# Head of a two-block transformer kernel: sums of squares and the first quarter of the modulation on TensorE, both factors of x in one VectorE pass, later sums before the second mixer

## The chip, the core and the metric

The kernel runs on 1 NeuronCore of one Trainium2 chip. The metric is device time in microseconds (us) of one execution; less is better. The engines named below are TensorE (PE in the profile; its weight loads are PEld), VectorE (DVE), ScalarE (ACT), GpSimd (POOL) and SyncE (SP), whose queue issues most of the transfers from memory.

## The reference, cut to what matters

Two transformer blocks run one after the other on 512 tokens of 1024 channels. What the change touches is the very first step, the normalised and modulated input of the first mixer, and the first product with it; and, far later, the norm that stands before the second mixer of the second block.

```python
c_act = jax.nn.silu(c)
mod = c_act @ ada_w[l] + ada_b[l]                 # 1024 -> 6 * 1024
shift1, scale1, gate1, shift2, scale2, gate2 = jnp.split(mod, 6)
h = rmsnorm(x, norm1_g[l]) * (1.0 + scale1) + shift1      # x: 512 x 1024
proj = h @ w_in[l]
...
def rms_norm(x, g):
    y = x * lax.rsqrt(jnp.mean(x * x, axis=-1, keepdims=True) + EPS)
    return y * g
...
x = x + rms_norm(sq_relu_mlp(h, ...), norm_mlp_post[0])   # second block, layer 0
m = mixer_c(rms_norm(x, norm_mix_pre[1]), ...)            # layer 1
```

## The kernel before, in words

Tokens lie along the free dimension and channels on the 128 partitions, so x is eight chunks (k = 0 to 7) of 128 channels by 512 tokens. Every product is made of three float32r matmuls: a weight slab and the activations are each split into a high part (a rounded copy, made on ACT) and a low part (the rest, made on DVE), and `mm3` issues high by high, high by low and low by high. A split of a weight slab is one ACT cast (`w_hi`, L168) and one DVE subtraction (`w_lo`, L169) of 128x1024.

**The head** is `first_products`. In it the order on every engine is the order in which the code is written (`manual_schedule`). It loads x and the columns of `ada_w` that give shift1 and scale1, in four quarters q: a quarter is eight tiles of 128x512 (k = 0 to 7, two to a buffer of 128x1024) and gives shift and scale for the chunks 2q and 2q+1. `ada` multiplies a quarter's tiles by c_act on DVE and adds them up over k; `columns` sums the result over the partitions with matmuls of one column (four for each 128x512 tile, 128x128 float32 weights, a column of ones as the moving side), and makes the factors `mod`. The squares of x are made on ACT, added up over k on DVE (L648) and summed over the partitions by four matmuls (`col_sum`, L326); the square root is a power on POOL (L344, `rs_r`); four matmuls `spread` it to 128 partitions (L353) and ACT copies it out (`rstd`, L356). Then x is multiplied by rstd (L654, chunk 0 on DVE, the others on POOL), by its scale factor on ACT (L636), and the shift is added while it is split in h_hi (ACT, L638) and h_lo (DVE, L639).

The first five products then grow side by side in five PSUM tiles: two slabs, the narrow forget slab `fa`, two more slabs. `mm(n, q)` adds slab n's share of quarter q, six matmuls of 512 columns. After slab number `NAT` of a quarter the next quarter's columns and factors stand in PE's order.

One float32 matmul leaves two records in the trace: "x8" in a row of L326, L353, L628 or L1320 is four matmuls.

**Before the second mixer** the last MLP product of layer 0 is made in two halves of 256 tokens (`halves`). The tail of a half (`post`) is woven between the matmuls of what follows, one step for each step or two of the other work: it makes the sums of squares of the new x (DVE, L283), then waits `late` steps, then sums them over the partitions on PE (L326, `csum`), takes the power on POOL (L1552, `mix_rcol`) and, two steps later, spreads it on PE (L1557). `LATE[1]` holds the late steps of the first and of the second half. POOL also adds the squares of the MLP's output m (L283 on POOL) in this stretch, and the scheduler orders this part itself.

Of the kernel before, what the change touches and what calls it, by code (L numbers as in the profile page):

```python
# [9 lines left out]
F32 = mybir.dt.float32  # L10
# [3 lines left out]
AF = mybir.ActivationFunctionType  # L14
OP = mybir.AluOpType
# [4 lines left out]
P = 128  # L20
S = 512
# [28 lines left out]
RATE = 1.0  # L50
APB = 2
EV = 1000
NPE = 0
NAT = 1
GY = 2
VK = 1
PK = 1
# [1 line left out]
R1 = 0.4  # L59
R5 = 0.4  # L60
APP = 0
LATE = ((40, 22), (34, 10))

# [19 lines left out]
class Net:  # L83
# [503 lines left out]
    def first_products(self, w, evacs, tmp, nf, rows):  # L587

        nc = self.nc
        with ExitStack() as es:  # L590
            sp = self.pool(es, "start", side="right")
            self.dense(es, 4)
            pp = self.pool(es, "pstart", 3, space=PSUM)
            more = [lambda: sp.tile([P, self.WN], F32, name="more_raw", bufs=2)] * 2
            self.weights_extra(self.zraw + more)
            self.parts.extend(self.pairs(sp, 2))
            E = mybir.EngineType
            es.enter_context(self.tc.manual_schedule(engines={E.PE, E.DVE, E.Activation, E.SP, E.Pool}))
# [12 lines left out]

            def ada(raws):
                acc = [sp.tile([P, 512], F32, name="ada_sum", bufs=4) for i in range(2)]
                for k in range(NC - NPE):
                    ck, a = self.c_act[:, k:k + 1], acc[k % 2]
                    if k < 2:
                        nc.vector.tensor_scalar(a, raws[k], ck, None, op0=OP.mult)
                    else:
                        nc.vector.scalar_tensor_tensor(a, raws[k], ck, a, op0=OP.mult, op1=OP.add)
                nc.vector.tensor_add(acc[0], acc[0], acc[1])  # L620
                return acc[:1]

            def columns(q, raws, acc):
                src = [(raws[k], self.c_act[:, k:k + 1]) for k in range(NC - NPE, NC)]
                for l, r in src + [(a, self.ones[:, :1]) for a in acc]:
                    for c in range(4):
                        d = 8 * (c // 2) + 2 * q + c % 2
                        nc.tensor.matmul(pa[:, d:d + 1], l[:, c * P:(c + 1) * P], r, start=False, stop=True,  # L628
                                         skip_group_check=True)
                for k in (2 * q, 2 * q + 1):  # L630
                    nc.scalar.mul(self.mod[:, 8 + k:9 + k], pa[:, 8 + k:9 + k], self.v("norm1_g", k))
                nc.scalar.copy(self.mod[:, 2 * q:2 * q + 2], pa[:, 2 * q:2 * q + 2])

            def modulate(q):
                for k in (2 * q, 2 * q + 1):
                    nc.scalar.mul(x[:, k], x[:, k], self.mod[:, 8 + k:9 + k])  # L636
                    b = self.mod[:, k:k + 1]
                    nc.scalar.activation(self.h[0][:, k], x[:, k], AF.Identity, bias=b)  # L638
                    nc.vector.scalar_tensor_tensor(self.h[1][:, k], x[:, k], b, self.h[0][:, k], op0=OP.add,  # L639
                                                   op1=OP.subtract)  # L640

            raws = [fetch(0)]
            acc = sp.tile([P, S], F32, name="acc", tag="ada_sum", bufs=4)
            nc.scalar.square(acc, x[:, 0])
            for k in range(1, NC):
                sq = sp.tile([P, S], F32, name="sq", bufs=2)
                nc.scalar.square(sq, x[:, k])
                nc.vector.tensor_add(acc, acc, sq)  # L648
            c = sp.tile([P, 4], F32, name="rs_c")
            nc.scalar.activation(c, self.col_sum([acc]), AF.Identity, bias=self.eps, scale=1.0 / D)  # L650
            r = self.spread(self.rsqrt(c), sp)
            sums = [ada(raws[0])]
            for k in range(NC):
                (nc.gpsimd if k else nc.vector).tensor_mul(x[:, k], x[:, k], r)  # L654
            slabs = [self.slab(w[i], NC) for i in range(2)]
            raw = sp.tile([P, NC * 16], F32, name="fa_raw")
            nc.sync.dma_start(raw, self.t["w_fa"])
            fa = tuple(sp.tile([P, NC, 16], F32R, name=n) for n in ("fa_h", "fa_l"))
            rv = raw.rearrange("p (k c) -> p k c", k=NC)
            nc.scalar.copy(fa[0], rv)  # L660
            nc.vector.tensor_sub(fa[1], rv, fa[0])
            slabs.append(fa)
            raws.append(fetch(1))
            columns(0, raws[0], sums[0])
            modulate(0)
            sums.append(ada(raws[1]))
            slabs += [self.slab(w[i], NC) for i in (2, 3)]
# [8 lines left out]
            for q in range(4):  # L676
                if q < 2:
                    raws.append(fetch(q + 2))
                    sums.append(ada(raws[q + 2]))
                for n in range(5):  # L680
                    if q < 3:
                        mm(n, q)
                        if n == NAT:
                            columns(q + 1, raws[q + 1], sums[q + 1])
                            modulate(q + 1)
# [1615 lines left out]
```

## Time and profile before

| | |
|---|---|
| time before, median of 3 runs | 2283.05 us (2279.7 to 2284.46) |
| profiled execution, its own time | 2282.78 us |
| its span | 2281.1 us |
| instructions | 31923 |
| mean granted TensorE clock | 0.975 |
| busy share: PE, DVE, ACT, POOL | 95%, 61%, 49%, 19% |

The span is the stretch between the first and the last instruction, and about 1.7 us of the execution's time lie outside it. Shares are means over a long kernel of many stages; the head is its first 69 us, 3% of the span.

### The profile page before, as it was taken

What the parts mean: (1) busy time and instruction counts of PE and PEld (TensorE: products, weight loads), DVE (VectorE), ACT (ScalarE), POOL (GpSimd) and SP (SyncE); (2) the same over time, 40 slices, a digit from 0 to 9 for tenths busy, and PEclk for the clock granted to TensorE, in tenths of its full rate; (3) what the DMA queues carried; (4) which work ended last, traced back from release to release, by engine and by line L of the source; (5) the groups of instructions that cost most, each with busy time, mean ns of one, the idle gap of its engine ahead of it and who ended that gap; (6) DMA issues with size and microseconds to landing.
All of it is one profiled execution on the core that took longest, in us unless ns stands there. A gap on an engine that the chain in (4) does not pass through costs nothing. (4 is left out here: it accounts for less than half of the span.)

```text
span 2281.1 us, 31923 instructions
## 1 busy us (share of the span) xinstructions
PE 2167.1 (95%) x12164; PEld 1809.7 (79%) x12164; DVE 1393.0 (61%) x2002; ACT 1109.9 (49%) x1856; POOL 422.6 (19%) x468
## 2 busy tenths in 40 slices
PE   5999999979999999899999999999999999999996
PEld 4778778967888788678998888997666689888886
DVE  8577775568999964666543344565767846344343
ACT  3545542348888854445553233443655647332231
POOL 4111000231111142110400000350324433000004
PEclk9999999989999989999999999999999999999998
DMA  6464265569999741224332222342122142332321
GB/s 242 140 185 118 88 204 164 184 223 345 353 358 355 270 154 45 69 78 151 100 111 97 98 94 100 110 135 55 49 71 54 43 158 89 117 101 93 101 74 38
DMA packets 127154, 320.08 MB, mean 140 GB/s; under 512 B 24751, under 2 KB 30127, under 8 KB 126994
## 3 DMA queue, kind: packets, MB, share of 16 engines
q1 hardware_dynamic: 111934, 286.56, 36.8%
q0 software_dynamic: 11200, 22.91, 4.2%
q10 hardware_dynamic: 3860, 8.51, 1.0%
q8 instruction: 97, 1.59, 0.3%
q14 instruction: 63, 0.52, 0.1%
HBM read 296.31 MB, written 18.69 MB: 138 GB/s over the span
## 5 line engine op out<-in xcount | busy, mean ns | idle before, releaser
L196 PE MATMUL acc<-h_hi,w_hi 128*128 128x512 f32 (+1 forms) x1464 | 515.7, 352 | 3.5 <-DVE q L429 1.5
L200 PE MATMUL acc<-h_hi,w_lo 128*128 128x512 f32 (+1 forms) x1464 | 509.1, 348 | 1.2 <-DVE w_lo L169 1.2
L199 PE MATMUL acc<-h_lo,w_hi 128*128 128x512 f32 (+1 forms) x1464 | 508.7, 348 | 0.0
L169 DVE TENSOR_TENSOR w_lo<-x_raw,w_hi 128x1024 fp32r<-128x1024 f32 x260 | 317.8, 1231 | 189.8 <-ACT w_hi L168 185.2
L168 ACT CAST w_hi<-x_raw 128x1024 fp32r<-128x1024 f32 x260 | 271.0, 1046 | 283.8 <-PE acc L199 246.6
L196 PEld LDWEIGHTS acc<-h_hi,w_hi 128*128 128x128 f32 x1464 | 279.5, 191 | 36.9 <-issue 2.7
L200 PEld LDWEIGHTS acc<-h_hi,w_lo 128*128 128x128 f32 x1464 | 278.9, 190 | 35.9 <-DVE w_lo L169 2.5
L199 PEld LDWEIGHTS acc<-h_lo,w_hi 128*128 128x128 f32 x1464 | 279.0, 191 | 29.7 <-issue 0.7
L169 DVE TENSOR_TENSOR w_lo<-w_raw,w_hi 128x1024 fp32r<-128x1024 f32 (+2 forms) x141 | 166.8, 1184 | 145.0 <-ACT w_hi L168 141.3
L168 ACT CAST w_hi<-w_raw 128x1024 fp32r<-128x1024 f32 (+2 forms) x141 | 143.6, 1019 | 222.1 <-PE acc L199 199.3
L196 PE MATMUL acc<-act_hi,w_hi 128*128 128x512 f32 (+1 forms) x640 | 223.0, 349 | 0.0
L199 PE MATMUL acc<-act_lo,w_hi 128*128 128x512 f32 (+1 forms) x640 | 222.6, 348 | 0.0
L200 PE MATMUL acc<-act_hi,w_lo 128*128 128x512 f32 (+1 forms) x640 | 222.4, 348 | 0.0
L283 POOL TENSOR_TENSOR acc<-acc,sq 128x256 f32<-128x256 f32 x60 | 55.5, 926 | 721.0 <-ACT sq L282 720.2
L196 PEld LDWEIGHTS acc<-act_hi,w_hi 128*128 128x128 f32 x640 | 121.9, 190 | 15.3 <-ACT act_hi L1621 0.3
L199 PEld LDWEIGHTS acc<-act_lo,w_hi 128*128 128x128 f32 x640 | 121.9, 190 | 15.0
L200 PEld LDWEIGHTS acc<-act_hi,w_lo 128*128 128x128 f32 x640 | 121.8, 190 | 15.0
L506 DVE TENSOR_TENSOR pl<-pexp,ph 128x512 fp32r<-128x512 f32 x144 | 113.9, 803 | 25.9 <-ACT ph L505 25.1
L1626 DVE TENSOR_TENSOR m<-m,acc 128x512 f32<-128x512 f32 (+1 forms) x64 | 35.2, 552 | 138.7 <-PE acc L200 138.7
L470 DVE TENSOR_REDUCE mx<-acc 128x1 f32<-128x128 f32 x192 | 89.2, 484 | 37.9 <-PE acc L469 36.3
L504 ACT ACTIVATE pexp<-sT 128x512 f32<-128x512 f32 x144 | 82.5, 573 | 32.2 <-PE sT L495 14.2
L196 PE MATMUL gu<-w_hi,xh 128*128 128x512 f32 x240 | 95.5, 398 | 0.0
(593 smaller groups left out, 4422.0 us busy)
## 6 DMA issues: line engine op xcount, KB each, us to landing
x_raw<-mlp_w SPq DMA_DIRECT2D x90, 512.0 KB
w_raw<-mlp_w SPq DMA_DIRECT2D x48, 512.0 KB
x_raw<-w_down SPq DMA_DIRECT2D x40, 512.0 KB
x_raw<-w_up SPq DMA_DIRECT2D x39, 512.0 KB
x_raw<-w_gate SPq DMA_DIRECT2D x38, 512.0 KB
w_raw<-w_in SPq DMA_DIRECT2D x20, 512.0 KB
h_raw<-w_up SPq DMA_DIRECT2D x19, 512.0 KB
h_raw<-w_gate SPq DMA_DIRECT2D x18, 512.0 KB
```

What stands on the lines that cost most here:

```text
L168: nc.scalar.copy(hi[:, :n], raw[:, :n])
L169: (eng or nc.vector).tensor_sub(lo[:, :n], raw[:, :n], hi[:, :n])
L196: mm(ps, l[0], r[0], start=start, stop=False)
L199: mm(ps, l[0], r[1], start=False, stop=False)
L200: return mm(ps, l[1], r[0], start=False, stop=stop).ins
L283: (eng or nc.gpsimd).tensor_add(acc[:, a:a + 256], acc[:, a:a + 256], sq)
L470: self.last_max = nc.vector.reduce_max(mx[:, c0 + qb:c0 + qb + 1], ps[:, :n], axis=AX.X).ins
L504: nc.scalar.activation(e[:, :o], ps[:, :o], AF.Exp)
L506: nc.vector.tensor_sub(pt[1][:, :o], e[:, :o], pt[0][:, :o])
L1626: nc.vector.tensor_add(self.m[:, i, tok], self.m[:, i, tok], ps)
```

## The change

At the head, PE sums the squares of each chunk as ACT makes it (32 matmuls of one column that add in one PSUM tile, which a matmul with zeros opens), and PE makes the whole first quarter of the modulation from the raw tiles (c_act as the moving column), half of it ahead of the spread and half behind it. DVE multiplies x by the scale factor and rstd in one instruction (`scale`); the passes on POOL and ACT are gone. Of the later quarters PE takes three of eight tiles raw (`NPE = 3`) and DVE five. `NAT` becomes one number for each quarter, the factors and splits of the next two chunks stand behind `columns`, and the next quarter's DVE sums behind them. The slabs 2 and 3 are loaded ahead of quarter 1. Before the second mixer the late steps go from 34 and 10 to 44 and 14.

```diff
-NPE = 0
-NAT = 1
+NPE = 3
+NAT = (3, 2, 2)
-LATE = ((40, 22), (34, 10))
+LATE = ((40, 22), (44, 14))
...
-            def columns(q, raws, acc):
-                src = [(raws[k], self.c_act[:, k:k + 1]) for k in range(NC - NPE, NC)]
-                for l, r in src + [(a, self.ones[:, :1]) for a in acc]:
+            def columns(q, raws, ks, acc=()):
+                for l, r in [(raws[k], self.c_act[:, k:k + 1]) for k in ks] + [(a, self.ones[:, :1]) for a in acc]:
...
-            def modulate(q):
-                for k in (2 * q, 2 * q + 1):
-                    nc.scalar.mul(x[:, k], x[:, k], self.mod[:, 8 + k:9 + k])
...
+            def scale(k):
+                nc.vector.scalar_tensor_tensor(x[:, k], x[:, k], self.mod[:, 8 + k:9 + k], r, op0=OP.mult, op1=OP.mult)
...
-            for k in range(1, NC):
+            cs = self.pn.tile([P, S], F32, name="csum", tag=self.ntags[0])[:, :4]
+            nc.tensor.matmul(cs, self.zb, self.zb[:, :4], start=True, stop=True)
+            for k in range(NC):
                 sq = sp.tile([P, S], F32, name="sq", bufs=2)
                 nc.scalar.square(sq, x[:, k])
-                nc.vector.tensor_add(acc, acc, sq)
+                for j in range(4):
+                    nc.tensor.matmul(cs[:, j:j + 1], sq[:, j * P:(j + 1) * P], self.ones[:, :1], start=False, stop=True,
+                                     skip_group_check=True)
...
-            sums = [ada(raws[0])]
-            for k in range(NC):
-                (nc.gpsimd if k else nc.vector).tensor_mul(x[:, k], x[:, k], r)
-            slabs = [self.slab(w[i], NC) for i in range(2)]
+            columns(0, raws[0], range(4))
+            r = self.spread(c, sp)
+            columns(0, raws[0], range(4, NC))
+            mods(0)
+            scale(0)
+            scale(1)
+            parts(0)
+            slabs = [self.slab(w[0], NC)]
+            parts(1)
+            slabs.append(self.slab(w[1], NC))
...
+                    mm(n, q)
+                    if n == NAT[q]:
+                        columns(q + 1, raws[q + 1], range(NC - NPE, NC), sums)
+                        mods(q + 1)
+                        for k in (2 * q + 2, 2 * q + 3):
+                            scale(k)
+                            parts(k)
+                        if q < 2:
+                            sums = ada(raws[q + 2])
```

On PE, at the start of the program, the difference of the two orders reads as follows; csum holds the sums of squares, w_raw and x_raw the raw tiles of the first quarter, ada_sum the sums that DVE made, pst the first product.

```order
 L602 MATMUL acc<-ones,idf 128x8
-L326 MATMUL csum<-ones,acc 128x1 x4
+L646 LDWEIGHTS zb
+L646 MATMUL csum<-zb 128x4
+L651 MATMUL csum<-ones,sq 128x1 x32
+L627 MATMUL acc<-c_act,w_raw 128x1 x16
 L353 MATMUL spread<-idf,rs_r 128x128 x4
-L628 MATMUL acc<-ones,ada_sum 128x1 x4
+L627 MATMUL acc<-c_act,x_raw 128x1 x16
 L196 MATMUL pst<-h_hi,w_hi 128x512
```

Ahead of the first product stood 12 matmuls of one column or 128, now there are 68, and the spread stands behind 16 of them.

On DVE, in the order of the changed kernel alone, this is what stands between the constants and the sums for quarter 2 (L636 is the multiplication by both factors, L641 the low part of h, L617 to L620 the sums of a quarter).

```order
L636 SCALAR_TENSOR_TENSOR x<-x,mod,rstd 128x512 x2
L641 SCALAR_TENSOR_TENSOR h_lo<-x,mod,h_hi 128x512
L169 TENSOR_TENSOR w_lo<-x_raw,w_hi 128x1024
L641 SCALAR_TENSOR_TENSOR h_lo<-x,mod,h_hi 128x512
L169 TENSOR_TENSOR w_lo<-x_raw,w_hi 128x1024
...
L620 TENSOR_TENSOR ada_sum<-ada_sum 128x512
L636 SCALAR_TENSOR_TENSOR x<-x,mod,rstd 128x512
L641 SCALAR_TENSOR_TENSOR h_lo<-x,mod,h_hi 128x512
L636 SCALAR_TENSOR_TENSOR x<-x,mod,rstd 128x512
L641 SCALAR_TENSOR_TENSOR h_lo<-x,mod,h_hi 128x512
```

In the later quarters the scaling of the second chunk stands behind the low part of the first, which waits for ACT's high part.

On POOL, before the second mixer, the first half's power (mix_rcol) stood here between the sums of squares of m (acc<-acc,sq); this is the order before:

```order
L1498 DMA x_dram<-x 128x8x256
L283 TENSOR_TENSOR acc<-acc,sq 128x256 x3
L1552 TENSOR_TENSOR mix_rcol<-rs_c,mh 128x2
L283 TENSOR_TENSOR acc<-acc,sq 128x256 x2
L1763 MEMSET v_hi 128x32
```

and this the order of the changed kernel, where its line is L1563:

```order
L1509 DMA x_dram<-x 128x8x256
L283 TENSOR_TENSOR acc<-acc,sq 128x256 x5
L1563 TENSOR_TENSOR mix_rcol<-rs_c,mh 128x2
L1774 MEMSET v_hi 128x32
```

Two more sums now stand ahead of the power. On PE, 30 more matmuls of 256 columns stand between the tail's first spread and these sums over the partitions (149, before 119), and 6 instead of 11 between them and the spread of the power; in the second half, 96 instead of 48 matmuls of the next product stand ahead of the first of these sums.

## Rows read from the trace of the kernel before

**Rows 1.** The page, busy time of each engine: busy us, share, instructions.
```profile
PE 2167.1 (95%) x12164; PEld 1809.7 (79%) x12164; DVE 1393.0 (61%) x2002; ACT 1109.9 (49%) x1856; POOL 422.6 (19%) x468
```
**Rows 2.** Waits of PE: us in total, times, longest.
```profile
PE csum L326 <- DVE acc L648: 10.3, 1, 10.3
...
PE csum L326 <- DVE acc L283: 5.1, 2, 3.1
...
PE acc L628 <- DVE ada_sum L620: 4.2, 1, 4.2
PE pst L199 <- DVE h_lo L639: 4.0, 2, 3.5
```
**Rows 3.** Timeline of PE, head: start, length, what, [idle before].
```profile
17.89 2.07 PE L353 MATMUL spread<-idf,rs_r 128*128 128x128 f32 x8 [1.81 <-POOL rs_r L344]
19.76 1.81 PE L628 MATMUL acc<-ones,ada_sum 128*128 128x1 f32 x8
24.47 0.80 PE L196 MATMUL pst<-h_hi,w_hi 128*128 128x512 f32 x1 [2.90 <-ACT h_hi L638]
...
33.35 0.40 PE L200 MATMUL pst<-h_hi,w_lo 128*128 128x512 f32 x1
...
39.69 0.59 PE L196 MATMUL pst<-h_hi,fa_h 128*16 128x512 f32 x1
...
49.05 0.95 PE L628 MATMUL acc<-ones,ada_sum 128*128 128x1 f32 x8
49.86 0.40 PE L196 MATMUL pst<-h_hi,fa_h 128*16 128x512 f32 x1
...
68.73 0.28 PE L196 MATMUL acc<-w_hi,h_hi 128*128 128x256 f32 x1
```
**Rows 4.** Windows, head: busy us of PE, PEld, DVE, ACT, POOL, then PEclk, DMA.
```profile
39.00:43.00 4.00, 4.00 (x12) 2.35 (x13) 4.00 (x8) 3.07 (x7) 0.00 (x0) 0.50 0.91 303
```
**Rows 5.** Timeline of the other engines, head.
```profile
5.80 0.63 ACT L644 ACTIVATE acc<-x 128x512 f32<-128x512 f32 x1 [2.77 <-DMA x<-x]
...
16.47 1.37 POOL L344 TENSOR_TENSOR rs_r<-rs_c,mh 128x4 f32<-128x4 f32 x1 [4.18 <-DMA x_raw<-w_in]
...
20.49 1.99 ACT L168 CAST w_hi<-x_raw 128x1024 fp32r<-128x1024 f32 x2
...
23.70 0.72 ACT L638 ACTIVATE h_hi<-x,mod 128x512 fp32r<-128x512 f32 x1
...
39.86 0.41 ACT L631 ACTIVATE mod<-acc,vec 128x1 f32<-128x1 f32 x2 [12.20 <-PE acc L628]
...
59.68 0.75 DVE L639 SCALAR_TENSOR_TENSOR h_lo<-x,mod,h_hi 128x512 fp32r<-128x512 f32 x1 [5.64 <-ACT h_hi L638]
...
65.79 1.23 DVE L169 TENSOR_TENSOR w_lo<-w_raw,w_hi 128x1024 fp32r<-128x1024 f32 x1 [1.64 <-ACT w_hi L168]
```
**Rows 6.** Timeline of PE in another stage: matmuls of two columns.
```profile
826.07 2.72 PE L1320 MATMUL gu<-gg,sq 128*128 128x2 f32 x12 [0.84 <-ACT sq L1318]
828.65 0.77 PE L1313 MATMUL acc<-kept 128*128 128x256 f32 x2
```
**Rows 7.** Windows of that stage, columns as in rows 4.
```profile
828.00:830.00 2.00, 2.00 (x11) 2.00 (x11) 0.54 (x2) 0.83 (x2) 0.00 (x0) 0.50 0.44 166
```
**Rows 8.** Timeline before the second mixer, PE, POOL and DVE.
```profile
1477.23 0.56 PE L326 MATMUL csum<-ones,acc 128*128 128x1 f32 x2 [3.08 <-DVE acc L283]
...
1479.73 1.54 POOL L283 TENSOR_TENSOR acc<-acc,sq 128x256 f32<-128x256 f32 x2 [0.19 <-ACT sq L282]
1481.22 0.71 POOL L1552 TENSOR_TENSOR mix_rcol<-rs_c,mh 128x2 f32<-128x2 f32 x1
...
1509.65 1.23 DVE L169 TENSOR_TENSOR w_lo<-w_raw,w_hi 128x1024 fp32r<-128x1024 f32 x1
```
**Rows 9.** Windows before the second mixer, columns as in rows 4.
```profile
1477.00:1484.00 7.00, 6.41 (x29) 6.14 (x30) 2.53 (x6) 2.18 (x7) 4.65 (x5) 0.52 0.86 281
1511.00:1518.00 7.00, 7.00 (x35) 6.92 (x34) 4.89 (x9) 2.65 (x7) 4.07 (x10) 0.51 0.91 271
```

More of the change, by code (lines that the diff above doesn't have):

```diff
@@ L612, in ada @@
             def ada(raws):
-                acc = [sp.tile([P, 512], F32, name="ada_sum", bufs=4) for i in range(2)]
+                acc = [sp.tile([P, S], F32, name="ada_sum", bufs=4) for i in range(2)]
                 for k in range(NC - NPE):
@@ L629, in columns, with mods @@
                                          skip_group_check=True)
+            def mods(q):
                 for k in (2 * q, 2 * q + 1):
@@ L632, in columns @@
                 nc.scalar.copy(self.mod[:, 2 * q:2 * q + 2], pa[:, 2 * q:2 * q + 2])
-            def modulate(q):
-                for k in (2 * q, 2 * q + 1):
-                    nc.scalar.mul(x[:, k], x[:, k], self.mod[:, 8 + k:9 + k])
[L637 to L640, printed above, removed]
+            def scale(k):
+                nc.vector.scalar_tensor_tensor(x[:, k], x[:, k], self.mod[:, 8 + k:9 + k], r, op0=OP.mult, op1=OP.mult)
@@ L642, in first_products, with parts @@
+            def parts(k):
+                b = self.mod[:, k:k + 1]
+                nc.scalar.activation(self.h[0][:, k], x[:, k], AF.Identity, bias=b)
+                nc.vector.scalar_tensor_tensor(self.h[1][:, k], x[:, k], b, self.h[0][:, k], op0=OP.add,
+                                               op1=OP.subtract)
             raws = [fetch(0)]
-            acc = sp.tile([P, S], F32, name="acc", tag="ada_sum", bufs=4)
-            nc.scalar.square(acc, x[:, 0])
-            for k in range(1, NC):
+            cs = self.pn.tile([P, S], F32, name="csum", tag=self.ntags[0])[:, :4]
@@ L646, in first_products @@
+            nc.tensor.matmul(cs, self.zb, self.zb[:, :4], start=True, stop=True)
+            for k in range(NC):
                 sq = sp.tile([P, S], F32, name="sq", bufs=2)
                 nc.scalar.square(sq, x[:, k])
-                nc.vector.tensor_add(acc, acc, sq)
+                for j in range(4):
+                    nc.tensor.matmul(cs[:, j:j + 1], sq[:, j * P:(j + 1) * P], self.ones[:, :1], start=False, stop=True,
+                                     skip_group_check=True)
             c = sp.tile([P, 4], F32, name="rs_c")
-            nc.scalar.activation(c, self.col_sum([acc]), AF.Identity, bias=self.eps, scale=1.0 / D)
@@ L651, in first_products @@
-            r = self.spread(self.rsqrt(c), sp)
-            sums = [ada(raws[0])]
-            for k in range(NC):
-                (nc.gpsimd if k else nc.vector).tensor_mul(x[:, k], x[:, k], r)
-            slabs = [self.slab(w[i], NC) for i in range(2)]
+            nc.scalar.activation(c, cs, AF.Identity, bias=self.eps, scale=1.0 / D)
+            c = self.rsqrt(c)
+            columns(0, raws[0], range(4))
+            r = self.spread(c, sp)
+            columns(0, raws[0], range(4, NC))
+            mods(0)
@@ L662, in first_products @@
             slabs.append(fa)
+            slabs += [self.slab(w[i], NC) for i in (2, 3)]
             raws.append(fetch(1))
[L664 to L667, printed above, removed]
+            sums = ada(raws[1])
             ps = [pp.tile([P, S], F32, name="pst") for _ in range(3)] + [self.ptile() for _ in range(2)]
@@ L674, in mm @@
                              k == NC - 1)
-            for q in range(4):
+            for q in range(3):
                 if q < 2:
                     raws.append(fetch(q + 2))
-                    sums.append(ada(raws[q + 2]))
                 for n in range(5):
[L681 to L685, printed above, removed]
+                    mm(n, q)
[7 more added lines that the diff above has]
+                            sums = ada(raws[q + 2])
             mm(2, 3)
```

## The prediction

> **What bounds the kernel now.** I read the page first: PE is busy 95% of the span [rows 1], so the kernel is as long as PE's work plus PE's waits, and what other engines save counts only where PE waits for them. So PE's waits came next [rows 2]. In the first 69 us it waits 10.3 us for the sums of squares, 4.2 for the sums of the modulation and 3.5 for one low part; far later it waits 3.1 and 2.0 us for the sums before the second mixer. These are what the change could remove. Then I read PE's timeline of the head [rows 3]. The first product's first matmul starts at 24.47; its first twelve matmuls are done at 33.75 (33.35 + 0.40); PE goes on at 39.69, and from there it is nearly gapless until the head ends at 68.73. So after 39.69 nothing but PE's own work counts, and before it the chain of x, of its norm and of the first factors. Last I read windows for the granted clock. TensorE runs at 0.50 (1.2 GHz) from 39 to 43 [rows 4], and in two stretches of 7 us behind the waits before the second mixer [rows 9].
>
> The sum is made against the profiled execution, 2282.78 us; the median of the three runs is 2283.05, 0.3 above it.
>
> **Prices.** Four float32 matmuls of one or two columns leave 8 records. At 1.2 GHz twelve records of two columns take 828.65 − 826.07 = 2.58 us [rows 6], the clock being 0.50 [rows 7]: 0.215 each. At full clock the 8 records before 49.86 take 0.81 [rows 3]: 0.10 each. In the head the page has no record of a throttle, but the first quarter's 8 records take 1.81 and the spread's 8 take 19.76 − 17.89 = 1.87 [rows 3], so the head starts at 1.2 GHz whatever its window prints. A product matmul of 512 columns takes (68.73 − 49.86) / 81 slots, that is 78 of them and one block of 8 records (0.81): 0.23 us; twice that, 0.46, at 1.2 GHz.
>
> **Head, up to the first products.** New on PE are 32 matmuls for the squares (64 records), 16 for the quarter's first half (32) and 16 for its second half (32); gone are four and four. The first square is ready at 5.80 + 0.63 = 6.43 [rows 5]. ACT makes one in 0.63, while PE needs 8 × 0.215 = 1.72 for a chunk, so PE sets the pace: 6.5 + 64 × 0.215 = 20.3. The first half of the columns follows, to 27.2; the power on POOL (1.37, rows 5) hides under it. Spread 1.87, to 29.05. Second half 6.9, to 35.9. Now the first factors, 0.45 after the columns (two at 0.41 overlap, rows 5); the scaling of chunk 0, taken at 0.75 as the other DVE pass of that form and size; the high part 0.72; and the cast of the first slab, 1.0 (two in 1.99), which stands behind it on ACT [rows 5]: 38.9, say **39.0**, against 24.47 now. The twelve first matmuls then take 12 × 0.46 = 5.6, to 44.6, where before went on at 39.69. **+4.9**. It is not +14.5, because the old start ran into the late second quarter: of the 15.2 us from 24.47 to 39.69 the new head needs 5.6.
>
> What is taken away here (the three waits of rows 2 and seven passes of x on POOL) is therefore already in the sum. The transfers of quarter 1 stand on SP behind the buffers that the first columns free (27 to 36); their first reader comes after 44.6, so I cost them at nothing; if that cover is too short, each us late is a us on PE.
>
> **Head, the three later column blocks.** Each is now 16 matmuls, 32 records at 0.10 = 3.25, where before had 8 records, 0.81, and only two of these blocks behind 39.69: 3 × 3.25 − 2 × 0.81 = **+8.1**. They are on PE's path, since PE is nearly gapless there; what they relieve, the sums on DVE, had slack by then.
>
> **Head, waits behind the blocks.** Scaling now stands behind the columns; before, ACT and POOL had it done. With E the end of a block, by 0.45, 0.75 and 0.72 the chunk's high part comes at E + 2.0 and its low part at E + 2.8; the second chunk's scaling stands on DVE behind that low part, so its parts come at E + 4.2 and E + 5.0, and the six matmuls of the next quarter's first slab end at about E + 5.4. The slabs left after a block cover part of it: one slab and the narrow one by NAT = 3 would end unstalled at E + 2.8, two with NAT = 2 at E + 4.2. Left are 2.6, 1.2 and 1.2 us, less the 0.5 that before waited: **+4.5**. Bounds: 0, if DVE and ACT are faster by overlap, to 7, if the w_lo splits (1.23 each, rows 5) stand ahead of them.
>
> **Clock.** Before pays 3.3 us at half clock behind 39.69 [rows 4], some 1.7 us lost. The new head will have been warmed by its first dense matmuls sooner, but each thin block and its wait may put it back, 1.7 at most each: **+0.5**, from −1 to +4. Head in all: **+18**.
>
> **Before the second mixer.** Thirty matmuls of 256 columns fill the wait of 3.1, and the sums are reached at about 1477.6, no later than now [rows 8]. But the power stands on POOL behind two more sums of 0.77: 1481.22 + 1.54 = 1482.8 [rows 8], and only six matmuls of PE stand between the sums and the spread of that power. So the wait moves to the spread (about 4 us from 1478.9 on, less what the thirty give back): gain 0 to 3. In the second half 48 more matmuls stand ahead of the sums, but they belong to a slab whose low part ends at 1510.88 on DVE [rows 8], when PE arrives at about 1507: it waits there as it waited for the sums. Gain 0 to 3.5. The half-clock stretches, 7 us each, about 3.3 lost in each [rows 9], stay as long as a wait stays in each place. I take **−2.5**; the bounds are +1 and −11.8 (both waits, 5.1, and both stretches, 6.7).
>
> **Sum:** 4.9 + 8.1 + 4.5 + 0.5 − 2.5 = +15.5, that is 2298.3; I say 2298.5. Its own range is 2293 to 2304.
>
> **The rivals.**
> *The thin stream raises the clock* (not slower). If the one-column matmuls of the squares lift TensorE to 2.4 GHz by about 12 us, squares end by about 12 (ACT then sets the pace) and columns cost 0.10 a record: the first product starts at about 25.5, twelve dense matmuls at full clock end near 30, and the next quarter, not PE, holds the head. I put its head at +2.5, with the mixer's −2.5: 2283, no change. It decides from a clock risen before 16 us on. Against it: from 826.07 PE is busy without a gap with two-column matmuls [rows 6], and 828 to 830, after 2 us of that, it still has 0.50 [rows 7]; rows 3's 8 records at 17.89 and at 19.76 are slow as well. For it: no row shows 14 us of such a stream.
> The Trainium skill, "TensorE: Matmul & The Clock Gate", section "Part 1: The HAM clock gate", says that the throttled state is the default and that activity of the array releases it; read so that 14 us of any matmuls are activity, it gives 2283, while the row gives 2298. The trace here agrees only for dense matmuls: behind 39.69 the clock rises at 43 [rows 4].
> *The whole gain of the mixer.* If the squares and slabs there come earlier because PE no longer holds their buffers, all 11.8 come back: 2282.78 + 18 − 11.8 = 2289. Against it stand the power on POOL and the slab's low part [rows 8].
> *The clock falls in every block.* If each of three thin blocks runs and ends at 0.50, each costs 3.3 more and its next dense matmuls up to 1.7: half of that on top, +6 to +7: 2304. For it speaks that rows 6 were thin and cold; against it that the 8 records at 49.05 ran at full clock [rows 3].
>
> **How the numbers follow.** Chances: the sum above 0.72; full gain of the mixer 0.11; thin stream warm 0.10; clock lost in each block 0.07. The range of 8 in 10 goes from 2288, which takes in the full gain of the mixer, to 2305, which takes in the blocks at half clock; the warm thin stream is left out below it. What the measurement can tell from no change is 0.2%, some 4.6 us: 2278.5 to 2287.6. Slower by more: the sum, the blocks, and nearly all of the mixer's case, 0.88; same: most of the warm stream, 0.07; faster, the warm stream together with some of the mixer's gain, 0.05.
>
> **What would show it.** In the changed profile: the last matmul of the squares near 20, in steps of about 1.7 a chunk; the spread at 27 to 29; the first product near 39; the head's end at 85 to 89 instead of 68.73; each column block 3.2 to 3.5; waits of PE for h_hi or h_lo behind each; before the second mixer no wait for the sums but one for the spread's power, and half-clock stretches still there. Wrong would be: 8 records of the squares in 0.8 (the clock rises early), a head end below 80, or no wait left before the second mixer.

## The result, and the profile after

The changed kernel takes 2301.33 us (median of 8 runs, 2296.57 to 2316.28), the kernel before 2283.09 (8 runs). By the medians it is slower by 18.2 us, 1.0080 times as long, inside the range of the prediction (2288 to 2305) and 2.8 above its 2298.5. The ratio on record, which weighs all the runs and is the one given for every kernel below, is 1.0091, 95% interval 1.0071 to 1.0110: two runs of 2312 and 2316 us lift it.

The page of the changed kernel has a span of 2299.6 us, 18.5 more than before, in which PE is busy 32 us longer [rows 1]:

```profile
span 2299.6 us, 32243 instructions
PE 2199.2 (96%) x12349; PEld 1842.5 (80%) x12349; DVE 1377.0 (60%) x1984; ACT 1105.1 (48%) x1848; POOL 411.1 (18%) x461
```

PE's waits, to be held against [rows 2]: the sums of squares and of the modulation are gone from the list, and so is the wait for the sums before the second mixer. In its place stands one for the power that is spread there. The other two are the factors, scaling and cast ahead of the first product (2.9) and the arrival of the first square (2.5). No wait came up for the transfers of quarter 1, which the prediction costed at nothing.

```profile
PE spread L1568 <- POOL mix_rcol L1563: 6.4, 2, 5.9
...
PE pst L196 <- ACT w_hi L168: 2.9, 1, 2.9
...
PE csum L651 <- ACT sq L649: 2.5, 1, 2.5
```

PE's timeline of the head, to be held against [rows 3]. In these rows a block of sixteen thin matmuls is written as 24 and 8 records (three raw tiles, then the sums):

```profile
6.45 13.81 PE L651 MATMUL csum<-ones,sq 128*128 128x1 f32 x64 [2.52 <-ACT sq L649]
20.13 6.97 PE L627 MATMUL acc<-c_act,w_raw 128*128 128x1 f32 x32
26.95 2.05 PE L353 MATMUL spread<-idf,rs_r 128*128 128x128 f32 x8
28.80 6.83 PE L627 MATMUL acc<-c_act,x_raw 128*128 128x1 f32 x32
38.51 0.80 PE L196 MATMUL pst<-h_hi,w_hi 128*128 128x512 f32 x1 [2.89 <-ACT w_hi L168]
...
43.20 0.40 PE L196 MATMUL pst<-h_hi,fa_h 128*16 128x512 f32 x1
...
46.00 2.73 PE L627 MATMUL acc<-c_act,x_raw 128*128 128x1 f32 x24
48.59 1.63 PE L627 MATMUL acc<-ones,ada_sum 128*128 128x1 f32 x8
50.09 0.77 PE L196 MATMUL acc<-h_hi,w_hi 128*128 128x512 f32 x1
...
85.38 0.28 PE L196 MATMUL acc<-w_hi,h_hi 128*128 128x256 f32 x1
```

The reader is to see three things. From 6.45 to 35.6 PE does thin matmuls almost without a gap (the second columns end at 28.80 + 6.83), and 64 records take 13.68 us, 0.214 each: half clock from the first to the last. (Windows print a clock of 1.00 there, since the profile has no record of it before 42 us; the half clock is read from the price, 0.215 a record at 0.50 [rows 6, rows 7].) The spread stands behind 48 of the thin matmuls, 32 of the squares and 16 of the columns. The first product starts at 38.51 instead of 24.47. And the head's last stage, the first matmul of 256 columns, starts at 85.38 instead of 68.73: +16.65.

Windows of the later quarters (busy us of PE, PEld, DVE, ACT, POOL, then granted clock and DMA) show what the first block does to the clock. It rises while dense matmuls run, is full when the block begins at 46.00, and is 0.50 when its sums run at 49:

```profile
42.00:46.00 4.00, 4.00 (x19) 2.63 (x18) 4.00 (x6) 0.11 (x1) 0.00 (x0) 1.00 0.89 260
46.00:49.00 3.00, 3.00 (x28) 3.00 (x27) 1.46 (x3) 0.00 (x0) 0.00 (x0) 0.97 0.94 300
49.00:50.00 1.00, 1.00 (x6) 1.00 (x6) 0.00 (x0) 0.00 (x0) 0.00 (x0) 0.50 1.03 422
50.00:55.00 5.00, 4.89 (x12) 3.09 (x11) 2.80 (x4) 1.91 (x5) 0.00 (x0) 0.50 0.77 300
...
62.00:66.00 4.00, 4.00 (x14) 3.18 (x14) 2.17 (x3) 1.45 (x5) 0.00 (x0) 0.57 0.00 0
```

To follow the difference through the program, I number the matmuls of the products (lines L196, L199 and L200, 9144 in either kernel) and subtract their starts. This **lag** is 14.0 us at the first, 16.65 at number 120 (head's end), 12.7 at number 600, 15.6 at number 2000, 15.5 at number 6060 (1468.2 before, 1483.7 after, ahead of the second mixer), 16.9 at number 6400 (1527.3 and 1544.3, behind it) and 18.5 at number 9000. So 16.65 came in the head and 1.4 at the second mixer. Elsewhere the lag falls by 3.9 and rises by 4.4 in places that the change doesn't touch. That is drift from execution to execution: three kernels below have the head of before (the late steps alone, and the two of the section on the power), they reach number 120 within 0.03 us of it, and number 600 at −1.9, −2.7 and +0.5. A trace is one execution, so a lag of 2 or 3 us far behind an edit proves nothing by itself.

### The profile page after: what moved, and what is told of

Same layout as the page of the kernel before. It is cut to its first block, busy times and chain, and to the rows that moved or that the text cites. A ratio compares the mean times of both kernels' runs of the same rounds, so it can differ in the third digit from the quotient of the medians.

```text
span 2299.6 us, 32243 instructions
## 1 busy us (share of the span) xinstructions
PE 2199.2 (96%) x12349; PEld 1842.5 (80%) x12349; DVE 1377.0 (60%) x1984; ACT 1105.1 (48%) x1848; POOL 411.1 (18%) x461
## 5 line engine op out<-in xcount | busy, mean ns | idle before, releaser
L196 PE MATMUL acc<-h_hi,w_hi 128*128 128x512 f32 (+1 forms) x1464 | 517.5, 354 | 3.3 <-DVE q L429 1.3
L200 PE MATMUL acc<-h_hi,w_lo 128*128 128x512 f32 (+1 forms) x1464 | 510.3, 349 | 1.4 <-DVE w_lo L169 1.4
L199 PE MATMUL acc<-h_lo,w_hi 128*128 128x512 f32 (+1 forms) x1464 | 509.8, 348 | 0.0
L169 DVE TENSOR_TENSOR w_lo<-x_raw,w_hi 128x1024 fp32r<-128x1024 f32 (+1 forms) x258 | 313.8, 1224 | 188.9 <-ACT w_hi L168 184.0
L168 ACT CAST w_hi<-x_raw 128x1024 fp32r<-128x1024 f32 (+1 forms) x258 | 269.1, 1046 | 284.7 <-PE acc L199 240.5
L196 PEld LDWEIGHTS acc<-h_hi,w_hi 128*128 128x128 f32 x1464 | 280.8, 192 | 36.2 <-issue 2.5
L200 PEld LDWEIGHTS acc<-h_hi,w_lo 128*128 128x128 f32 x1464 | 280.2, 191 | 36.0 <-DVE w_lo L169 2.7
L199 PEld LDWEIGHTS acc<-h_lo,w_hi 128*128 128x128 f32 x1464 | 280.5, 192 | 29.5 <-issue 0.7
L169 DVE TENSOR_TENSOR w_lo<-w_raw,w_hi 128x1024 fp32r<-128x1024 f32 (+2 forms) x141 | 166.8, 1184 | 143.3 <-ACT w_hi L168 141.3
L196 PE MATMUL acc<-act_hi,w_hi 128*128 128x512 f32 (+1 forms) x640 | 222.3, 348 | 0.0
L199 PE MATMUL acc<-act_lo,w_hi 128*128 128x512 f32 (+1 forms) x640 | 221.9, 347 | 0.0
L200 PE MATMUL acc<-act_hi,w_lo 128*128 128x512 f32 (+1 forms) x640 | 221.7, 347 | 0.0
L196 PEld LDWEIGHTS acc<-act_hi,w_hi 128*128 128x128 f32 x640 | 121.2, 189 | 15.3 <-ACT act_hi L1632 0.3
L199 PEld LDWEIGHTS acc<-act_lo,w_hi 128*128 128x128 f32 x640 | 121.2, 189 | 15.0
L200 PEld LDWEIGHTS acc<-act_hi,w_lo 128*128 128x128 f32 x640 | 121.2, 189 | 15.0
L196 PE MATMUL gu<-w_hi,xh 128*128 128x512 f32 x240 | 95.2, 397 | 0.0
```

Of the source, the lines that this page charges most:

```text
L168: nc.scalar.copy(hi[:, :n], raw[:, :n])
L169: (eng or nc.vector).tensor_sub(lo[:, :n], raw[:, :n], hi[:, :n])
L196: mm(ps, l[0], r[0], start=start, stop=False)
L199: mm(ps, l[0], r[1], start=False, stop=False)
L200: return mm(ps, l[1], r[0], start=False, stop=stop).ins
```

## The experiments

Twelve kernels ran, in four groups; each is compared with the kernel before on the same chip, whose median was 2284.3 to 2286.0 in these groups. So ratios are compared across groups, not microseconds. A lag is always against the profiled execution of before.

### The late steps, taken out and alone

In the changed kernel:

```diff
-LATE = ((40, 22), (44, 14))
+LATE = ((40, 22), (34, 10))
```

> The changed kernel with the late steps before the second mixer back at 34 and 10; the head is the changed one. Theory: the later sums cost a little, since the wait only moved to the power on POOL (5.9 us there in the changed kernel, where the kernel before waited 3.1 and 2.0 for the sums); the aligned product matmuls lost 1.3 us in this place, so this kernel is 1.3 below the changed one: 2300.0, 17 above before. Rival, as forecast: the later sums gain 2.5, and taking them away costs it: 2303.8. In both the head ends at 85.4.

Measured: 2305.4, ratio 1.0091 (1.0073 to 1.0110), the same as the changed kernel. Its head's end lags by 16.3. In time the late steps can't be seen here: the theory's 1.3 us and the rival's 2.5 are both less than the interval, some 4 us to either side.

In the kernel before:

```diff
-LATE = ((40, 22), (34, 10))
+LATE = ((40, 22), (44, 14))
```

> The kernel before with only the late steps at 44 and 14. Theory: 1.3 us slower than before, 2284.4, with a wait of about 6 us at the spread of the power in place of 3.1 at the sums. Rival, as forecast: 2.5 faster, 2280.6. Third: all of the waits and the half clock come back, 11.8 faster, 2271.3.

Measured: 2289.13, ratio 1.0022 (1.0007 to 1.0038): a little slower, and neither rival. The wait at the spread of the power is 5.9 as in the changed kernel, and the lag grows by 1.43 from matmul 6060 to 6400. (The ratio is worth 5 us; another 3.9 of lag come between 6600 and 7000, where other kernels drift as far and further.) The reason for the wait stands on VectorE and POOL, in the timelines of this kernel:

```profile
1479.98 0.15 DVE L337 TENSOR_SCALAR rs_c<-csum 128x2 f32<-128x2 f32 x1
```
```profile
1478.51 1.81 POOL L283 TENSOR_TENSOR acc<-acc,sq 128x256 f32<-128x256 f32 x1 [1.67 <-ACT sq L282]
1480.85 0.72 POOL L283 TENSOR_TENSOR acc<-acc,sq 128x256 f32<-128x256 f32 x1 [0.53 <-ACT sq L282]
1482.10 0.72 POOL L283 TENSOR_TENSOR acc<-acc,sq 128x256 f32<-128x256 f32 x1 [0.53 <-ACT sq L282]
1483.35 0.72 POOL L283 TENSOR_TENSOR acc<-acc,sq 128x256 f32<-128x256 f32 x1 [0.53 <-ACT sq L282]
1484.60 0.72 POOL L283 TENSOR_TENSOR acc<-acc,sq 128x256 f32<-128x256 f32 x1 [0.53 <-ACT sq L282]
1485.28 0.71 POOL L1552 TENSOR_TENSOR mix_rcol<-rs_c,mh 128x2 f32<-128x2 f32 x1
```

From the second on there is a sum every 1.25 us, 0.72 of work and 0.53 of waiting for ScalarE's next square: square and sum take turns. What the power works on (rs_c) is ready at 1480.13, but the power stands behind all the sums in POOL's order and starts at 1485.28.

### The first quarter's clock, and where the blocks' cost goes

The first of these adds dense matmuls, whose results nobody reads, among the thin ones of the changed kernel:

```diff
+            wb = self.h[0][:, 7, :256].bitcast(BF)
+            nc.vector.memset(wb, 1.0)
+            def warm(n):
+                for _ in range(n):
+                    nc.tensor.matmul(wp, wb[:, :P], wb, start=True, stop=True)
+            warm(10)
...
+                warm(2)
```

The pairs of `warm(2)` stand behind each chunk's squares and behind each tile of the first quarter.

> The changed kernel with additional dense matmuls of 512 bf16 columns on a tile of ones, whose results nobody reads: ten before the first matmul of the program, two behind each chunk's squares and two behind each raw tile of the first quarter. Theory (what makes the head late is that the thin matmuls run at half clock): eight records take 0.8 instead of 1.72, the squares end at 16.5 and not at 20.2 although 16 matmuls more stand among them, the first product starts at about 30 instead of 38.5 and at full clock; head -10, 2291. Rival (dense matmuls among them do not lift or hold the clock): each pair adds 0.85, first product at about 52, 2313. Third (the clock is lifted, but the raw tiles or quarter 1 hold the head): first product near 30 and the head's end back near 85, 2300.

Measured: 2307.0, ratio 1.0112 (1.0091 to 1.0133), first product at 46.2. The windows show the theory holding for 5 us and then failing:

```profile
4.00:8.00 4.00, 4.00 (x21) 2.69 (x20) 0.90 (x4) 1.23 (x3) 4.00 (x5) 1.00 0.94 347
8.00:10.00 2.00, 2.00 (x19) 1.83 (x17) 0.00 (x0) 1.17 (x2) 2.00 (x3) 1.00 1.05 409
10.00:12.00 2.00, 2.00 (x11) 1.63 (x10) 0.00 (x0) 0.63 (x1) 2.00 (x3) 0.55 1.05 424
12.00:16.00 4.00, 4.00 (x19) 3.27 (x18) 0.00 (x0) 1.26 (x2) 0.21 (x2) 0.50 1.03 410
```

Ten dense matmuls lifted the clock, the next chunks' eight records took 0.8 to 0.9 instead of 1.72, and with two dense matmuls to eight thin records the clock fell again near 10 and stayed at 0.50 until 44. So the three fast chunks show that half clock doubles the price of the thin records; that a head at full clock would be early is not shown, since this mix doesn't hold the clock and the added matmuls then cost 0.8 a pair. At 0.8 a chunk TensorE is still slower than ScalarE's 0.63 for a square, so in the rival of the warm stream ScalarE would not have set the pace.

The second takes the raw tiles out of quarters 1 to 3:

```diff
-NPE = 3
+NPE = 0
```

> The changed kernel with all eight tiles of quarters 1 to 3 summed on VectorE (NPE = 0); the first quarter stays raw on TensorE. Theory (the thin blocks are paid on TensorE's path, and they drop its clock): three blocks shrink by 2.4 us each and the dips of 3.1 and 2.0 us behind two of them go, less waits for VectorE, which has 2.1 us more sums for each quarter: about -8, 2293, blocks of 0.8 to 0.9 us and full clock behind them. Rival (VectorE becomes the bound, its sums come later than the blocks by 2 to 3.5 us each): 2301, with waits for ada_sum that take up the gain.

Measured: 2306.61, ratio 1.0103 (1.0082 to 1.0124), head's end lag 16.6. The rival: with the sums written behind the scaling, VectorE is late in every quarter, and the waits in the head take up all that the shorter blocks give.

```profile
PE acc L627 <- DVE ada_sum L620: 5.6, 3, 2.5
```

The clock falls in this head too, with blocks of only eight thin records behind waits of 1.1 to 2.5 us: the granted clock is 0.66 from 50 to 55 and 0.58 from 60 to 65.

The third leaves the blocks' work as it is and spreads it among the dense matmuls:

```diff
             def mm(n, q, cols=()):
                 hi, lo = slabs[n]
                 for k in (2 * q, 2 * q + 1):
+                    for c in cols[k % 2:k % 2 + 1]:
+                        columns(*c)
...
-                        columns(q + 1, raws[q + 1], range(NC - NPE, NC), sums)
```

> The changed kernel with the columns of quarters 1 to 3 spread among the dense matmuls ahead of them, four thin matmuls to every six dense ones, instead of sixteen in one block. The work is the same. Theory (the block drops the clock, which costs 12 and 9 product matmuls at half clock and the end of two blocks, about 5 us): full clock after 42, no product matmul at half clock in the later quarters, head's end near 80.5, 2296. Rival (thin matmuls among dense ones drop the clock all the same, or the raw tiles are late when they stand earlier): half clock stays, 2301.

The kernel has four thin matmuls (eight records) to every three dense ones, not to every six. Measured: full clock from 43 to 83, and no product matmul at half clock there, as the theory has it:

```profile
43.00:50.00 7.00, 7.00 (x50) 5.92 (x49) 4.93 (x8) 0.47 (x3) 0.00 (x0) 1.00 0.91 307
50.00:55.00 5.00, 3.73 (x17) 2.26 (x15) 3.36 (x7) 1.45 (x2) 0.00 (x0) 1.00 0.73 297
55.00:65.00 10.00, 9.90 (x57) 7.72 (x57) 5.24 (x8) 1.91 (x5) 0.00 (x0) 1.00 0.01 2
```

The head's end comes at 82.35, 3.0 earlier than in the changed kernel and not 5; PE reaches the next chunks sooner and now waits 2.0 us for h_hi and h_lo where it waited 0.9 (the gap in the second row). In time nothing of it is seen: 2305.8, ratio 1.0091 (1.0073 to 1.0109). But 3.0 us are 0.13%, less than the interval to either side. Its lag grows from 13.6 to 16.2 between matmul 120 and 600, in work that the edit doesn't touch; that is within the drift of that stretch.

### The parts of the head, apart

Sums of squares back on VectorE, raw columns of the first quarter on TensorE around them:

```diff
...
+                nc.vector.tensor_add(acc, acc, sq)
+            columns(0, raws[0], (0, 1))
+            cs = self.col_sum([acc])
...
-            columns(0, raws[0], range(4))
+            columns(0, raws[0], (2, 3))
```

> The changed kernel with the sums of squares back on VectorE (seven additions and four matmuls, as before); TensorE makes only the raw columns of the first quarter, two tiles ahead of the sum over the partitions, two behind it, four behind the spread. Theory (the 64 records of the squares at half clock are what stands first on the path): TensorE's first stretch shrinks from 132 to 80 records and begins when the raw tiles land, near 10: 17.5 us of work, first product at about 30.6 instead of 38.5; 2293, the head's end near 77.5. Rival (raw tiles land too late, or the quarter behind it holds the head): first product earlier, but the head's end at 83 to 85: 2300.

Measured: 2297.21, ratio 1.0053 (1.0033 to 1.0072), so the squares are worth some 0.4% of the 0.9%. The first product starts at 31.20 (theory 30.6):

```profile
11.12 3.54 PE L627 MATMUL acc<-c_act,w_raw 128*128 128x1 f32 x16 [7.19 <-DMA w_raw<-ada_s]
14.53 1.84 PE L326 MATMUL csum<-ones,acc 128*128 128x1 f32 x8
...
21.49 6.83 PE L627 MATMUL acc<-c_act,x_raw 128*128 128x1 f32 x32
31.20 0.80 PE L196 MATMUL pst<-h_hi,w_hi 128*128 128x512 f32 x1 [2.89 <-ACT w_hi L168]
```

but the head's end only at 81.68, 3.7 earlier than in the changed kernel, between theory (77.5) and rival. Of the 7.3 us gained, 1.0 is lost in the first twelve products and 2.6 in the blocks and behind them: here all three drop the clock (0.61 from 44 to 48, 0.50 from 56 to 60 and from 68 to 72), where in the changed kernel the third did not.

The scaling alone, on the kernel before:

```diff
-                    nc.scalar.mul(x[:, k], x[:, k], self.mod[:, 8 + k:9 + k])
+                    nc.vector.scalar_tensor_tensor(x[:, k], x[:, k], self.mod[:, 8 + k:9 + k], r, op0=OP.mult, op1=OP.mult)
+                for k in (2 * q, 2 * q + 1):
...
-            for k in range(NC):
-                (nc.gpsimd if k else nc.vector).tensor_mul(x[:, k], x[:, k], r)
```

> The kernel before with one part of the change alone: VectorE scales x by both factors in one instruction, both chunks ahead of their splits; POOL's and ScalarE's passes are gone, everything else is as before. Theory (POOL's seven passes slowed VectorE, w_lo took 2.1 us beside them and 1.23 alone): VectorE has quarter 1's sums some 4.4 us earlier, then it has 8.6 us of work in each quarter against 7.75 of TensorE and gives 2 us back: 2281, 2 faster than before. Rival A (VectorE becomes the bound in each quarter, and scaling stands behind the next sums): waits for h_hi of 2 us a quarter, 2286 to 2288. Rival B (quarter 1's transfers, not VectorE, set its sums): no gain at 39.69, 2285.

Measured: 2281.01, ratio 0.9981 (0.9968 to 0.9994): **faster** than before. The first product starts 1.2 later, and quarter 1's sums are ready much earlier, so that its block runs at 32.62; in the kernel before it runs at 37.96, the row by itself:

```profile
25.68 0.79 PE L196 MATMUL pst<-h_hi,w_hi 128*128 128x512 f32 x1 [4.09 <-ACT h_hi L639]
...
32.62 1.86 PE L628 MATMUL acc<-ones,ada_sum 128*128 128x1 f32 x8 [2.16 <-DVE ada_sum L620]
...
65.65 0.28 PE L196 MATMUL acc<-w_hi,h_hi 128*128 128x256 f32 x1
```
```profile
37.96 1.87 PE L628 MATMUL acc<-ones,ada_sum 128*128 128x1 f32 x8 [4.21 <-DVE ada_sum L620]
```

The head's end is 3.1 earlier than before. The groups of VectorE's lines from 20 to 69 (busy us, mean ns) say why, first in this kernel, then in the kernel before:

```profile
L169 DVE TENSOR_TENSOR w_lo<-x_raw,w_hi 128x1024 fp32r<-128x1024 f32 x4 | 4.7, 1220 | 1.9 <-ACT w_hi L168 1.9
```
```profile
L169 DVE TENSOR_TENSOR w_lo<-x_raw,w_hi 128x1024 fp32r<-128x1024 f32 x4 | 6.5, 1668 | 0.3 <-ACT w_hi L168 0.3
```

The same four instructions are 37% longer in the mean where POOL multiplies beside two of them. They are not the only ones: VectorE's work beside POOL (two each of L169, h_lo and L617, one of fa_l) takes 4.17, 3.43, 2.91 and 1.35 us in the kernel before and 2.36, 1.41, 0.87 and 0.28 in this one, 6.9 less, of which the new scaling takes back 1.41. The Trainium skill ("SBUF — State Buffer", section "SBUF: two separate sides") has VectorE and GpSimd share one port pair, of which one engine is shut out while the other's instruction holds it; the rows agree that VectorE lost time there.

And the raw tiles alone, added to that kernel:

```diff
-NPE = 0
+NPE = 3
```

> The run with the one-instruction scaling alone, and of it three tiles of every quarter raw on TensorE (NPE = 3): squares and five tiles stay on VectorE, NAT is 1, the block of a quarter is 32 records instead of 8. Theory (the blocks themselves are dear: 2.4 us each on TensorE's path, 5.2 at half clock in the first quarter, and they drop the clock): first product near 30, head's end near 74 to 77 instead of 65.6, 2290. Rival (VectorE is the bound of this head, and 2.1 us less of sums in each quarter pay for the block): head's end at or below 66, 2281.

Measured: 2293.18, ratio 1.0033 (1.0017 to 1.0049), 0.5% over the scaling alone. The theory, a little on the dear side: head's end at 78.21 (expected 74 to 77), 12.6 later, and in the first quarter three raw tiles at half clock:

```profile
19.77 5.12 PE L628 MATMUL acc<-c_act,x_raw 128*128 128x1 f32 x24
24.75 1.84 PE L628 MATMUL acc<-ones,ada_sum 128*128 128x1 f32 x8
28.54 0.80 PE L196 MATMUL pst<-h_hi,w_hi 128*128 128x512 f32 x1 [1.95 <-ACT h_hi L639]
```

### Before the second mixer: what the power waits for

Two kernels give the later sums of the first half another way past the sums of m. In both the late steps are 44 and 10, so the second half is as before; the diffs shown leave that line out. In one VectorE makes these sums from the fourth on:

```diff
-            self.sq_half(accs[hb], self.m[:, i, tok], seen[hb])
+            self.sq_half(accs[hb], self.m[:, i, tok], seen[hb], self.nc.vector if save and hb and seen[hb] > 2 else None)
```

> The kernel before with the first half's late steps at 44 (the second half stays at 10) and the sums of squares of m in the second half made by VectorE from the fourth on, so that the power on POOL no longer stands behind them. The head is that of before. Theory (the later sums gave nothing only because the power was queued behind five sums of m): the wait at the spread is 1 to 2 us instead of 5.9, 2280, some 4 faster than before. Rival (other things hold the stretch: VectorE takes on the delay, or the matmuls gained are lost again at the next slab): 2284 to 2286, as with the late steps alone.

Measured: 2283.01, ratio 0.9996 (0.9983 to 1.0009), no change. The wait at the spread is still 4.7: the power now stands alone on POOL, but what it works on, rs_c, is made by VectorE behind the same sums:

```profile
1481.43 0.43 DVE L283 TENSOR_TENSOR acc<-acc,sq 128x256 f32<-128x256 f32 x1 [0.48 <-ACT sq L282]
1482.34 0.42 DVE L283 TENSOR_TENSOR acc<-acc,sq 128x256 f32<-128x256 f32 x1 [0.48 <-ACT sq L282]
1482.68 0.15 DVE L337 TENSOR_SCALAR rs_c<-csum 128x2 f32<-128x2 f32 x1
```

In the other the sums stay on POOL, and the last square of x gets a buffer of its own (`last` is not "sq" there), so that two are left for the squares of m:

```diff
-            acc.append(self.np.tile([P, 256], F32, name="sq"))
+            acc.append(self.np.tile([P, 256], F32, name=last, **({"tag": "ap_t", "bufs": APB} if last != "sq" else {})))
```

> The kernel before with the first half's late steps at 44 (second half 10) and the last square of the new x of that half in a buffer of its own (it shares the one of ap_t), so that it no longer keeps one of the two sq buffers from the squares of m until TensorE has summed it. The five sums of m stay ahead of the power on POOL. Theory (each of those sums took 1.25 us because square and sum took turns in one free buffer, 0.72 and 0.53): with two buffers they run at 0.72 to 0.77, the power starts some 2.4 us earlier and the wait at the spread falls from 5.9 to about 3.5; 2281 to 2282. Rival (ScalarE's order or POOL's own rate sets the sums, not the buffer): wait of 5 to 6 as in the changed kernel, 2285.

Measured: 2280.75, ratio 0.9983 (0.9971 to 0.9995), faster. The wait at the spread is 3.4, the lag falls by 4.1 between matmul 6060 and 6400, and four of the sums now run in one stretch, 1.00 us each in the mean (three take 0.73; the one beside VectorE's low part of a slab takes 1.59):

```profile
1479.42 4.00 POOL L283 TENSOR_TENSOR acc<-acc,sq 128x256 f32<-128x256 f32 x4 [0.33 <-ACT sq L282]
1483.38 0.71 POOL L1553 TENSOR_TENSOR mix_rcol<-rs_c,mh 128x2 f32<-128x2 f32 x1
```

In the changed kernel TensorE has read the last square of x by 1494.0, and the turns still go on until 1499.3. So what counts seems to be the buffer that each square is given in the program's order, not which one is free at the time; this is argued, not shown.

### What can be made of it

The head with the scaling alone, the first two slabs split ahead of the copy of rstd, and half of the sums of quarters 2 and 3 behind the scaling:

```diff
-            r = self.spread(self.rsqrt(c), sp)
+            c = self.rsqrt(c)
             sums = [ada(raws[0])]
             slabs = [self.slab(w[i], NC) for i in range(2)]
+            r = self.spread(c, sp)
...
-                    sums.append(ada(raws[q + 2]))
+                    sums.append(ada(raws[q + 2], range(4)))
...
                             modulate(q + 1)
+                            if q < 2:
+                                sums[q + 2] = ada(raws[q + 2], range(4, NC), sums[q + 2])
```

> The kernel before with the one-instruction scaling on VectorE, as in the run of that part alone, and two orders changed: the first two slabs are split ahead of the copy of rstd (ScalarE and VectorE stood idle there), and of the sums of quarters 2 and 3 four passes stand behind the scaling of the quarter ahead instead of in front of it. Theory (after the first product VectorE is the bound of the head, so what it does earlier comes back whole): quarter 1's sums end 1.8 earlier and the wait of 1.2 for h_hi and h_lo at 42 goes; 3 us below the run with the scaling alone, head's end near 62.5, about 2278. Rival (the slabs' raw tiles land too late to be split earlier, or quarter 1's transfers set its sums): no change against that run, 2281.

Measured: 2280.49, ratio 0.9980 (0.9966 to 0.9994). In the trace the theory, first product at 23.66 and head's end at 62.61, 3.0 ahead of the scaling alone; in time no difference from it that the runs can tell, 3 us being less than the interval to either side.

Both together, this head and the buffer before the second mixer:

> The two edits that helped, together: the head with one-instruction scaling on VectorE and the earlier slabs, and before the second mixer late steps 44 and 10 with the last square in a buffer of its own. Theory (the places are 1400 us apart, so the gains add): head 6 us earlier, 3 to 4 us less before the second mixer, 8 to 10 in all, about 2276. Rival (what is gained at the head is spent where TensorE waits for transfers later on, as the runs of either part suggest by their smaller gain in time): 2280, no better than either part.

Measured: 2276.46, ratio 0.9960 (0.9944 to 0.9977). Within the intervals the gains add: the lag is −7.0 at the head's end and falls by 3.3 at the second mixer. This kernel is faster than the kernel before by 0.4%, and than the changed kernel by 1.3%.

## Why the prediction was right, and where not

**The head's first stretch was right step by step.** Squares end at 20.13 (forecast 20.3), spread at 26.95 (27.2), the columns' end at 35.63 (35.9), first product at 38.51 (39.0). The price of a thin record, read from another stage [rows 6], held for 128 of them. The not-slower rival, a stream that lifts the clock, is refuted by this row: 29 us of thin matmuls at 0.21 us a record. Of the Trainium skill's rule that activity releases the throttle ("TensorE: Matmul & The Clock Gate", section "Part 1: The HAM clock gate") this case bears out the half about dense matmuls; thin ones kept PE busy without a gap and released nothing, and the measurement decides.

**The head's sum was right, +16.65 against +18, its terms less so.** The resumption after the first twelve matmuls came at 43.20, +3.5 and not +4.9, since the clock rose at 42 while they ran. The blocks cost 4.09 + 3.49 + 3.49 = 11.07, less 1.62: +9.4, forecast 8.1; of the 1.3 between them, 0.6 is the first block's last eight records at half clock (1.50 us, 0.9 in the others), and the rest a record at 0.108 where the forecast had 0.10. The waits behind them were 0.9 and not 5.0, and the clock made up for part of it: 12 and 9 product matmuls behind two blocks took 5.63 and 3.73 us, 9.4 in place of 4.8 at 0.23 each. About 0.7 of the 5.63 is waiting too, hidden by the modelled ends of slow matmuls: the starts at 54.38 and 55.17 come 0.73 and 0.79 behind the one before, the others 0.43. The two terms hang together: slow matmuls leave scaling and splits the time to finish, and in the woven kernel, where the clock stays up, waits appear in their place. With the 0.5 and 1.7 that the prediction puts down for before, waits and clock come to 0.9 + 4.5 − 2.2 = 3.2 where the forecast had 4.5 + 0.5 = 5.0, and the head's terms to 3.5 + 9.4 + 3.2 = 16.1 of the 16.65. So that the head's sum is near is in part luck: 4.9 for 3.5 and 5.0 for 3.2 were too much, 8.1 for 9.4 too little.

**The second mixer's gain did not come.** The forecast was −2.5; in the profiled execution the lag rose by 1.4, 1.6 in the first half and −0.2 in the second. The second half went as told, at the low end of its 0 to 3.5: PE waits for the slab's low part as it waited 2.07 for the sums:

```profile
1528.76 0.39 PE L199 MATMUL acc<-w_lo,h_hi 128*128 128x256 f32 x1 [2.34 <-DVE w_lo L169]
```

In the first half the step that failed is "two more sums of 0.77: 1481.22 + 1.54 = 1482.8". The sums of m ran at one in 1.25 us there, not 0.77, because each takes turns with the square that feeds it; the power started at 1499.98, or 1484.5 with the lag of 15.5 taken off, and the wait at the spread was 5.9, not about 4. That the free buffer is what makes them take turns is shown by the kernel with one more (1.00 us each, wait 3.4, ratio 0.9983; its second half has 10 late steps and not 14). That the queue matters and not POOL as such is shown by the kernel that moved the sums to VectorE and took the wait along. How much the changed late steps cost in time, and whether they cost anything, is not settled: alone they gave 1.0022, taken out of the changed kernel nothing, and executions of kernels with the old late steps differ by −2.7 to +1.8 us in this stretch. What is shown is that the forecast gain is not there. In the total this miss of 3.9 us and the head's 1.35 the other way cancel in part, and that 2298.5 came within 3 us owes something to that.

**What the parts are worth,** by ratios: the scaling alone 0.9981; with three raw tiles a quarter 1.0033; with the whole first quarter raw, the new order and late steps, squares still on VectorE, 1.0053; with the squares on TensorE 1.0091. So the one part that took work off a waiting chain gained 0.2%, and the parts that gave TensorE thin work, with the new order and late steps, lost 1.1%. The step from 1.0033 to 1.0053 is inside the intervals, and no kernel has the new order alone.

**Not settled:** whether the 3 us that the woven kernel and the earlier slabs gain in the head reach the time; the runs can't tell so little.

## What to carry to other kernels

An engine that waits isn't free capacity if what it is given runs at a worse rate than what it waits for: the four thin matmuls of a tile take 0.8 us at full clock and 1.7 at half, and a block of them often drops the clock for the dense ones behind, against one pass of VectorE of 0.75, which in the later quarters was hidden (at 49.05 PE waits for no sum [rows 3]). Price moved work at the clock of the place it goes to, and look whether an engine beside it is slowed by what is taken away, since that was the gain here. Before a sum is put later to hide a wait, list what its successors queue behind, on which engine and with how many free buffers.

## What the runs showed of the hardware

- The clock fell in the midst of uninterrupted work: full at 46.00, 0.50 at 49, PE busy all the time, with thin matmuls. With one block of eight thin records to every three dense matmuls (the woven kernel) it stayed at 1.00 from 43 to 83; with eight to two of another kind (bf16, 512 columns, on a tile of ones) it fell to 0.50. Each is one trace.
- Which of three like blocks drops the clock differs from kernel to kernel: the first two in the changed kernel, all three with the squares on VectorE.
- The power on POOL took 1.37 us beside a busy VectorE [rows 5] and 1.04 in the changed kernel, where VectorE stands idle at that point.
